# A trunk kernel's lead-in written in another order: the first coefficient group between the two input halves, the second half's squares summed on GpSimd and TensorE

## The chip, the core and the metric

The kernel runs on one core of a Trainium2 chip. A core has TensorE (PE, matrix products into PSUM, with a sequencer of its own for loading weights, PEld), VectorE (DVE), ScalarE (ACT), GpSimd (POOL), and SyncE (SP), on whose queue the loads and stores of this kernel are issued. The metric is the device time of one execution in microseconds (us).

## The reference

The reference is a decoder trunk of two layers on one sequence of 1024 tokens with 1024 channels. A layer normalizes its input, scales and shifts it by coefficients from a conditioning vector `c`, projects it once into all branches, runs three token mixers (pooling, retention, RWKV-7), merges them by gates and projects back:

```python
    mod = c_act @ w_ada + b_ada                       # c_act = silu(c)
    shift, scale, gate = jnp.split(mod[:, None, :], 3, axis=-1)
    h = rms_norm(x, norm_g) * (1.0 + scale) + shift
    proj = h @ w_in
    ...
    merged = jnp.sum(gates * y, axis=2)
    return x + gate * (merged @ w_out)
```

Here `rms_norm` multiplies x by the reciprocal root of the mean of its squares over the channels and by `norm_g`. All that the change touches is the first of these steps in the first layer: the sums of squares, the coefficients `scale` and `shift`, the normalized input `h`, and the first products with `w_in`.

## The kernel before

**Layout.** Activations lie with channels on the partitions: x is eight tiles (`kt` = 0 to 7, 128 channels each) by two halves (`h` = 0, 1, 512 tokens each), so a tile is 128x512. Matrix products contract over `kt`. They are made of three products each at the fast format: an operand is split into a rounded high part and a low remainder (`hhi`, `hlo` for h; `wh`, `wl`, or the two parts of a `wbig` tile, for weights), and high x high, low x high and high x low are added in one PSUM tile. ScalarE casts the high part, GpSimd or DVE subtracts for the low part (`split`, L529 and L530; `affine` and `low`, L1171 to L1177).

**The lead-in** is everything from the start to the end of the first layer's first three weight tiles (the low-rank tile and the first `k` and `r` tile of RWKV-7). It is written by hand: in `with tc.manual_schedule(...)` the order of the text is the order of each of PE, DVE, ACT and POOL; SP's order is placed by the compiler around it, and follows the text but for loads moved up from behind. Its pieces:

- `xdma(h, ...)` loads the tiles of half h; `wdma(j, ...)` the raw weights of the three tiles (j is the half of the contraction); `aload(g, n)` loads weights of coefficient group g into a ring of eight slots.
- `sq(h, ...)`: ScalarE squares a tile (L1127), DVE adds it to the running sum (L1131). `sums(h)`: four matmuls of 128x1 add that over the partitions. `rstd(h)`: ScalarE's root (L1146) and DVE's reciprocal (L1147). `rstd_bc(h)`: four matmuls broadcast the reciprocal roots to all partitions in PSUM (`rbc`). `rstd_copy(h)`: ScalarE copies this to SBUF (`rbs`, L1157), since GpSimd multiplies from there. `normed(h, kt, ...)`: x times the broadcast, on DVE from `rbc` (L1163) or on GpSimd from `rbs` (L1165).
- The coefficients come in groups. Groups 0 to 3 are scale and shift of tiles 0 to 3, group 4 of tiles 4 and 5, group 5 of tiles 6 and 7 (groups 6 and 7, the gates, come later and elsewhere). A group is a generator, `ada` (L225 and L227): eight steps, one per contraction tile, each a DVE instruction that multiplies a loaded weight tile by a column of `cact` and adds it to a sum in PSUM. `steps(g, n)` runs the next n of them. The ninth step is PE's column sums (`adaps`, 128x1 matmuls) and `ada_end`: DVE adds the bias (`mod`, L244) and makes the scale (`acoef`, L250).
- `affine(h, kt)`: two ScalarE passes make the high part and the full h (L1171, L1172); `low` its remainder (L1177). `mms(h, kt, tiles)`: the nine matmuls of one kt for three weight tiles (or those named), into the accumulators `acc6[h]`; those of half 0 come from the pool of accumulators (`acc_ps`), those of half 1 from the pools `ch` and `cy`, which serve the chunk work later, and the broadcast `rbc` earlier.
- `derive(l)`: four small DVE instructions on a vector of layer parameters (`vec`, L179 to L185).

A tile's h thus needs its half's reciprocal root and its group's coefficients; its matmuls need h and the split weights.

**Behind the lead-in** nothing is written out by hand: a planner keeps lanes of tasks, estimates times in a clock of its own that each recorded matmul advances, and gives out work by due time. The first task there evacuates the lead-in's accumulators; `setup_rest` loads the remaining constants and runs `derive(1)`, and `rope_tables` makes the rotary tables.

Of the kernel before, what the change touches and what calls it, by code (L numbers as in the profile page):

```python
# [13 lines left out]
ALU = mybir.AluOpType  # L14
# [3 lines left out]
P = 128  # L18
# [78 lines left out]
def trunk_kernel(ctx, tc, xT, cvec, pos, vecs, consts, w_ada, w_all, pool_w, lora_w, out):  # L97
# [79 lines left out]
    def derive(l):  # L177
        o = VEC["mu_k"]
        nc.vector.tensor_scalar(omu[l], vec[l][:, o : o + 13], -1.0, 1.0, op0=ALU.mult, op1=ALU.add)  # L179
        halved = vec[l][:, VEC["pool_scale"] : VEC["mu_k"]]  # L180
        nc.vector.tensor_scalar_mul(halved, halved, 0.5)
        o = VEC["k_k"]
        nc.vector.tensor_scalar_mul(vec[l][:, o : o + 4], vec[l][:, o : o + 4], -1.0)
        o = VEC["k_a"]
        nc.vector.tensor_scalar(oka[l], vec[l][:, o : o + 4], -1.0, 1.0, op0=ALU.mult, op1=ALU.add)  # L185

    def setup_rest():
        o = CST["bone"]
        braw = mo("braw")[:, 0:P]
        nc.sync.dma_start(out=braw, in_=consts[:, o : o + P])  # L190
        nc.vector.tensor_copy(bone, braw)
        nc.sync.dma_start(out=vec[1], in_=vecs[1])
        derive(1)

    def vv(l, k, i):
        o = VEC[k] + i
# [15 lines left out]
    def ada(l, g, slot_, gap=2200, acc_=t_lt, ws=None):  # L212
# [47 lines left out]
    def rope_tables():  # L260
# [10 lines left out]
        for h in range(2):  # L271
# [22 lines left out]
                nc.sync.dma_start(out=rope_d[h, 64 * r : 64 * r + 64, :], in_=n[0:64, :])  # L294
            nc.sync.dma_start(out=rope_d[2, 64 * h : 64 * h + 64, :], in_=n[64:128, :])
            yield 6000

    xd = [dp.tile([8, 2, P, HF], F32, name=f"xd{l}") for l in range(1)]
    gd = dp.tile([3, 8, 2, P, HF], F32, name="gd")
# [819 lines left out]
            nc.sync.dma_start(out=xt, in_=xT[kt, h])  # L1119
            xin[h].append(xt)  # L1120

    ssum = [None, None]

    def sq(h, *kts):
        for kt in kts:
            t = t_lt("sq") if kt == 0 else mo("sq")
            nc.scalar.square(t, xin[h][kt])  # L1127
            if kt == 0:
                ssum[h] = t
            else:  # L1130
                nc.vector.tensor_tensor(ssum[h], ssum[h], t, op=ALU.add)  # L1131

    ssp = [None, None]

    def sums(h):
        ssp[h] = mx("ssps")
        for m in range(4):
            mmul(ssp[h][:, m : m + 1], ssum[h][:, m * P : (m + 1) * P], ones)

    rn_ = [None, None]  # L1140
    rbc = [None, None]
# [65 lines left out]
    with tc.manual_schedule(engines={ET.PE, ET.DVE, ET.Activation, ET.Pool}):  # L1207
# [4 lines left out]
        def aload(g, n):  # L1212
            ada_load(0, g, wada_slot, aw[g], n)
# [35 lines left out]
        sq(1, 7)  # L1249
        sums(1)  # L1250
        wsp(0, 0)
        normed(0, 4, eng=G_)
        normed(0, 1)
        steps(gs[0], 6)
        rstd(1)
        steps(gs[0], 3)
        aload(3, 2)
        rstd_bc(1)
        wsp(0, 1, 2)
        steps(gs[1], 2)  # L1260
        affine(0, 0)
        steps(gs[1], 1)
        normed(1, 0)
        low(V, 0, 0)
# [4 lines left out]
        steps(gs[1], 3)
        rstd_copy(1)  # L1270
        acc6[0] = [acc_ps() for _ in range(3)]
        mms(0, 0)
        normed(1, 2, 3)
        acc6[1] = [ps_c.tile([P, HF], F32, tag=t, name=nm("acc"), bufs=n) for t, n in (("ch", 1), ("cy", 2), ("cy", 2))]
        mms(1, 0, 0, 1)
        steps(gs[1], 1)
        mms(1, 0, 2)
        normed(0, 5, 6, eng=G_)
        both(1)
        wdma(1, 0, 1, 2)  # L1280
        aload(4, 6)
        steps(gs[2], 8)
        mms(0, 1)
        mms(1, 1, 0, 1)
        steps(gs[2], 1)
        mms(1, 1, 2)
        wsp(1, 0)
        normed(0, 7, eng=G_)
        both(2)
        steps(gs[3], 8)  # L1290
        aload(4, 2)
        mms(0, 2)
        mms(1, 2, 0, 1)
        steps(gs[3], 1)
        mms(1, 2, 2)
        wsp(1, 1)
        both(3)
        wsp(1, 2)
        normed(1, 4, eng=G_)
        astep(4, 5)  # L1300
        mms(0, 3)
        mms(1, 3, 0, 1)
        steps(gs[4], 1)
        mms(1, 3, 2)
        both(4)
        normed(1, 5, eng=G_)
        both(5)
        astep(5)
# [323 lines left out]
```

## Time and profile before

| | |
|---|---|
| Time before, median of 3 runs | 2500.98 us (2497.89 to 2501.22) |
| Profiled execution, its own time | 2501.75 us |
| Its span, from first to last instruction | 2499.9 us |
| Mean granted TensorE clock | 0.983 |
| PE busy, of the span | 2397.6 us, 96% |
| DVE, ACT, POOL busy | 1357.1, 791.9, 822.8 us |
| First matmul of a weight tile | at 27.6 us |
| Last matmul of the lead-in ends; next weight tile begins | 77.4 us |

Times of the trace run from the start of the span. An instruction belongs to a line of the kernel; where a helper issues it, as `mmul` does for every matmul (L411), the tile names tell which it is: `ssps` are the column sums of squares, `rbc` the broadcast, `adaps` the column sums of a coefficient group, `acc` the accumulators of weight tiles. Idle time ahead of an instruction is put down to what released it.

### The profile page before, as it was taken

Reading aid. Unit: us, or ns where it says so; the run is one execution under the profiler, and the core shown is the slowest. Engines: PE = TensorE matmul, PEld = TensorE weight load, DVE = VectorE, ACT = ScalarE, POOL = GpSimd, SP = SyncE. Lnnn points to the kernel's source line nnn. Section 1 sums busy time; section 2 is a strip of 40 time slices with the busy share of each in tenths; the row PEclk is TensorE's granted clock in tenths of the full one; section 3 lists DMA queues with packets and bytes.
Section 4 is the critical chain, followed back from the end, with each engine's and each line's share of the span. In section 5 each row is a group of like instructions: output and inputs, shape, how many; then the busy total and the mean of one; then the engine's idle time right before and its main releaser. Section 6 shows DMA issues by size and latency. Waiting matters only on the chain. (4 is left out here: it accounts for less than half of the span.)

```text
span 2499.9 us, 34854 instructions
## 1 busy us (share of the span) xinstructions
PE 2397.6 (96%) x13312; PEld 1980.1 (79%) x13312; DVE 1357.1 (54%) x2564; ACT 791.9 (32%) x1465; POOL 822.8 (33%) x721
## 2 busy tenths in 40 slices
PE   6989999999999999999999999999999999999998
PEld 4778878877787787887877787788878778787888
DVE  7674566478268443567445646835744664412354
ACT  5532332231332222112444224223322322221243
POOL 4221322232133234454442132322313323236441
PEclk9999999999899999999999999999999999999999
DMA  7131112112113215676431211211211121354342
GB/s 245 54 109 56 43 35 85 36 38 68 47 55 115 75 57 161 193 230 190 136 112 47 68 39 34 77 35 43 86 42 35 61 81 55 123 156 126 102 152 77
DMA packets 124216, 223.68 MB, mean 89 GB/s; under 512 B 14096, under 2 KB 17424, under 8 KB 124048
## 3 DMA queue, kind: packets, MB, share of 16 engines
q1 hardware_dynamic: 124048, 221.44, 28.4%
q8 instruction: 105, 1.72, 0.3%
q14 instruction: 63, 0.52, 0.1%
HBM read 174.46 MB, written 46.92 MB: 89 GB/s over the span
## 5 line engine op out<-in xcount | busy, mean ns | idle before, releaser
L530 POOL TENSOR_TENSOR wl<-wr,wh 128x512 fp32r<-128x512 f32 x342 | 453.6, 1326 | 1189.5 <-ACT wh L529 1108.7
L411 PE MATMUL acc<-hhi,wh 128*128 128x512 f32 x2000 | 809.0, 404 | 14.5 <-DVE k L997 11.1
L411 PE MATMUL acc<-hhi,wl 128*128 128x512 f32 x2000 | 808.5, 404 | 1.7 <-POOL r L991 1.7
L411 PE MATMUL acc<-hlo,wh 128*128 128x512 f32 x2000 | 809.8, 405 | 0.0
L411 PEld LDWEIGHTS acc<-hhi,wh 128*128 128x128 f32 x2000 | 381.1, 191 | 86.5 <-DVE k L997 12.7
L411 PEld LDWEIGHTS acc<-hhi,wl 128*128 128x128 f32 x2000 | 381.4, 191 | 71.7 <-issue 2.2
L411 PEld LDWEIGHTS acc<-hlo,wh 128*128 128x128 f32 x2000 | 381.9, 191 | 68.3 <-issue 0.7
L529 ACT CAST wh<-wr 128x512 fp32r<-128x512 f32 x342 | 211.8, 619 | 680.8 <-PE acc L411 471.5
L411 PE MATMUL acc<-olo,wh 128*128 128x512 f32 x384 | 153.5, 400 | 4.4 <-POOL olo L530 4.3
L411 PE MATMUL acc<-oG,wh 128*128 128x512 f32 x384 | 153.3, 400 | 2.0 <-ACT oG L529 1.0
L411 PE MATMUL acc<-oG,wl 128*128 128x512 f32 x384 | 152.0, 396 | 0.0
L942 DVE TENSOR_TENSOR xst<-cy,MT 64x128 f32<-64x128 f32 x128 | 36.2, 283 | 185.5 <-PE cy L411 185.0
L953 DVE SCALAR_TENSOR_TENSOR S<-ch,pc,SP 64x64 f32<-64x64 f32 x256 | 72.4, 283 | 95.0 <-PE ch L411 86.1
L881 DVE TENSOR_TENSOR MT<-MT,tm 64x30 f32<-64x30 f32 (+14 forms) x240 | 103.9, 433 | 7.5
L939 ACT ACTIVATE SP<-S,pc 128x128 f32<-128x128 f32 x128 | 51.4, 402 | 173.8 <-DVE S L953 169.3
L875 DVE TENSOR_TENSOR tm<-MT 64x30 f32<-64x30 f32 (+14 forms) x240 | 101.3, 422 | 7.5
L948 DVE COPY Z<-ch 64x128 f32<-64x128 f32 x128 | 36.1, 282 | 117.7 <-PE ch L411 117.3
L411 PEld LDWEIGHTS acc<-olo,wh 128*128 128x128 f32 x384 | 73.2, 191 | 22.6 <-POOL olo L530 6.6
L411 PEld LDWEIGHTS acc<-oG,wh 128*128 128x128 f32 x384 | 72.9, 190 | 20.9 <-ACT oG L529 2.0
L1457 DVE SCALAR_TENSOR_TENSOR gs<-gs,acc 128x512 f32<-128x512 f32 x64 | 43.5, 683 | 82.8 <-PE acc L411 71.7
L411 PEld LDWEIGHTS acc<-oG,wl 128*128 128x128 f32 x384 | 73.1, 190 | 16.8
L411 PEld LDWEIGHTS ch<-xst,G 128*128 128x128 f32 x512 | 76.7, 191 | 11.6 <-DVE xst L942 0.5
(273 smaller groups left out, 3643.8 us busy)
## 6 DMA issues: line engine op xcount, KB each, us to landing
wr<-in_w_all SPq DMA_DIRECT2D x364, 256.0 KB, 2.7
gd<-gsg SPq DMA_DIRECT2D x80, 256.0 KB, 2.0
gs<-gd SPq DMA_DIRECT2D x80, 256.0 KB, 2.9
wada<-in_w_ada SPq DMA_DIRECT2D x70, 256.0 KB, 3.1
ol<-od SPq DMA_DIRECT2D x64, 256.0 KB, 3.0
ringG<-in_w_ada SPq DMA_DIRECT2D x26, 256.0 KB, 5.2
x<-in_xT SPq DMA_DIRECT2D x16, 256.0 KB, 4.9
od<-po SPq DMA_DIRECT2D x16, 256.0 KB, 2.3
```

Source lines behind the costliest of these rows:

```text
L411: nc.tensor.matmul(out, lhsT=lhsT, rhs=rhs, start=start, stop=stop, **kw)
L529: nc.scalar.copy(hi, src)
L530: eng.tensor_tensor(lo, src, hi.bitcast(F32), op=ALU.subtract)
L875: nc.vector.tensor_tensor(pr, M3[:, i + 1 :, i : i + 1].to_broadcast([64, n, i]), M3[:, i : i + 1, 0:i].to_broadcast([64, n, i]), op=ALU.mult,
L881: nc.vector.tensor_tensor(M3[:, i + 1 :, 0:i], M3[:, i + 1 :, 0:i], pr, op=ALU.add)
L939: nc.scalar.activation(SP, S, AF.Copy, scale=pcc)
L942: nc.vector.tensor_tensor(xst[0:64, :], cy[0:64, 0:P], AV[:, c * P : (c + 1) * P], op=ALU.add)
L948: nc.vector.tensor_copy(Z[0:64, c, :], ch[0:64, 0:P])
L953: nc.vector.scalar_tensor_tensor(Sn[rw, rw], ch[rw, P + 64 * hd : P + 64 * hd + 64], pc[rw, c : c + 1], SP[rw, rw], op0=ALU.mult, op1=ALU.add,
L1457: nc.vector.scalar_tensor_tensor(s, s, 1.0, ps, op0=ALU.add, op1=ALU.mult)
```

## The change

Five things are done differently in the lead-in, and two small pieces of text are moved.

1. Loads: group 0's four weight tiles are issued ahead of half 1's eight input tiles; the first three raw weight tiles come together behind half 1.
2. Half 1's squares (`sq2`): ScalarE squares two tiles, GpSimd adds the pair, and PE adds the pair's column sums into one PSUM tile, four times. DVE makes half 0's sum alone. Both halves' sums go into tiles of the accumulators' pool.
3. Group 0 is computed between the halves. In `ada` a step is added between the column sums and `ada_end`, so that the next group's two first steps can be put between them, and they are for groups 1 to 5.
4. Normalization: tiles 2 and 3 of half 0 go from GpSimd to DVE; tiles 6 and 7 of half 1 from DVE to GpSimd; of tile 1, the low part of half 0 is on DVE. Tiles 6 and 7 of half 1 are normalized before the matmuls of tile 4, and no longer behind them.
5. Matmuls: half 0 and half 1 alternate to the end, where before tiles 6 and 7 of half 0 came first and then those of half 1; and they are less cut up by weight tile.

The load of the second layer's parameter vector and `derive(1)` are moved from `setup_rest` to the end of `rope_tables`. The diff, cut to its core:

```diff
@@ setup_rest, ada, rope_tables
-        nc.sync.dma_start(out=vec[1], in_=vecs[1])
-        derive(1)
...
             mmul(ps[:, m : m + 1], acc[:, m * P : (m + 1) * P], ones)
+        if not late:
+            yield
         ada_end(l, g, ps)
...
             yield 6000
+        nc.sync.dma_start(out=vec[1], in_=vecs[1])
+        derive(1)
@@ lead-in
-    def sq(h, *kts):
+    def sq(*kts):
...
-    def sums(h):
-        ssp[h] = mx("ssps")
+    def sums():
+        ssp[0] = acc_ps()
...
+    def sq2(j):
+        a, b = mo("sq"), t_lt("sq")
+        nc.scalar.square(a, xin[1][2 * j])
+        nc.scalar.square(b, xin[1][2 * j + 1])
+        nc.gpsimd.tensor_tensor(a, a, b, op=ALU.add)
+        if j == 0:
+            ssp[1] = acc_ps()
+        for m in range(4):
+            mmul(
+                ssp[1][:, m : m + 1], a[:, m * P : (m + 1) * P], ones,
+                start=(j == 0 and m == 0), stop=(j == 3 and m == 3), skip_group_check=True,
+            )
...
+        aload(0, 4)
         xdma(1, *range(8))
-        wdma(0, 0)
-        aload(0, 4)
-        wdma(0, 1, 2)
+        wdma(0, 0, 1, 2)
         aload(1, 4)
...
-        sq(0, *range(8))
-        sums(0)
-        sq(1, 0, 1, 2)
+        sq(*range(8))
+        sums()
+        steps(gs[0], 4)
+        sq2(0)
         rstd(0)
         rstd_bc(0)
         derive(0)
-        sq(1, 3, 4, 5, 6)
+        steps(gs[0], 4)
+        aload(3, 2)
+        sq2(1)
+        steps(gs[0], 1)
+        sq2(2)
+        steps(gs[0], 1)
         rstd_copy(0)
-        normed(0, 2, 3, eng=G_)
         normed(0, 0)
...
+        affine(0, 0)
         normed(0, 1)
-        steps(gs[0], 6)
+        sq2(3)
+        wsp(0, 0, 1, 2)
+        low(V, 0, 0)
+        normed(0, 2, 3)
+        steps(gs[1], 5)
         rstd(1)
...
         mms(0, 4)
         mms(1, 4)
-        normed(1, 6, 7, eng=V)
         mms(0, 5)
-        mms(1, 5, 0, 1)
         steps(gs[5], 1)
-        mms(1, 5, 2)
+        mms(1, 5)
+        steps(gs[5], 1)
         both(6, V)
         both(7, V)
         wprep(True)
         wprep()
         mms(0, 6)
+        mms(1, 6)
         mms(0, 7)
-        mms(1, 6)
         mms(1, 7)
```

**How the instructions now stand.** DVE, from the last addition to half 0's sum (`sq_183`) on; before:

```order
L1131 TENSOR_TENSOR sq_183<-sq_183,sq_203 128x512
L1131 TENSOR_TENSOR sq_211<-sq_211,sq_213 128x512
L1131 TENSOR_TENSOR sq_211<-sq_211,sq_216 128x512
L1147 RECIPROCAL rn_219<-rn_219 128x4
L179 TENSOR_SCALAR omu_103<-vec_91 128x13
L181 TENSOR_SCALAR vec_91<-vec_91 128x28
L183 TENSOR_SCALAR vec_91<-vec_91 128x4
L185 TENSOR_SCALAR oka_105<-vec_91 128x4
L1131 TENSOR_TENSOR sq_211<-sq_211,sq_231 128x512
L1131 TENSOR_TENSOR sq_211<-sq_211,sq_234 128x512
L1131 TENSOR_TENSOR sq_211<-sq_211,sq_237 128x512
L1131 TENSOR_TENSOR sq_211<-sq_211,sq_240 128x512
```

and with the change:

```order
L1134 TENSOR_TENSOR sq_183<-sq_183,sq_203 128x512
L223 TENSOR_SCALAR ada_ps_212<-ringG_137,cact 128x256
L225 SCALAR_TENSOR_TENSOR ada_ps_212<-ringG_137,cact,ada_ps_212 128x256 x3
L1161 RECIPROCAL rn_227<-rn_227 128x4
L179 TENSOR_SCALAR omu_103<-vec_91 128x13
L181 TENSOR_SCALAR vec_91<-vec_91 128x28
L183 TENSOR_SCALAR vec_91<-vec_91 128x4
L185 TENSOR_SCALAR oka_105<-vec_91 128x4
L225 SCALAR_TENSOR_TENSOR ada_ps_212<-ringG_137,cact,ada_ps_212 128x256 x3
L225 SCALAR_TENSOR_TENSOR ada_acc_211<-ringG_137,cact,ada_ps_212 128x256
L244 TENSOR_TENSOR mod_99<-adaps_254,vec_91 128x2
L250 SCALAR_TENSOR_TENSOR acoef_101<-mod_99,vec_91 128x1
```

Half 1's additions (`sq_211`) are gone from DVE; four of group 0's steps stand ahead of half 0's reciprocal and four behind `derive(0)`, and group 0's coefficient (`mod_99`, `acoef_101`) ahead of the first normalization.

PE from its first instruction; before:

```order
L411 MATMUL ssps_206<-fixed,sq_183 128x1 x4
L411 MATMUL rbc_222<-cst,rn_219 128x128 x4
L411 MATMUL ssps_251<-fixed,sq_211 128x1 x4
L411 MATMUL adaps_273<-fixed,ada_acc_260 128x1 x2
L411 MATMUL rbc_280<-cst,rn_268 128x128 x4
L411 MATMUL acc_313<-hhi_293,wbig_153 128x512 x2
```

and with the change (`acc_206` and `acc_222` are the halves' column sums now):

```order
L413 MATMUL acc_206<-fixed,sq_183 128x1 x4
L413 MATMUL acc_222<-fixed,sq_217 128x1 x4
L413 MATMUL rbc_230<-cst,rn_227 128x128 x4
L413 MATMUL acc_222<-fixed,sq_245 128x1 x4
L413 MATMUL adaps_254<-fixed,ada_acc_211 128x1 x2
L413 MATMUL acc_222<-fixed,sq_257 128x1 x4
L413 MATMUL acc_222<-fixed,sq_276 128x1 x4
L413 MATMUL acc_319<-hhi_271,wbig_158 128x512 x2
L413 MATMUL acc_319<-hlo_272,wbig_158 128x512
L413 MATMUL rbc_325<-cst,rn_301 128x128 x4
L413 MATMUL adaps_330<-fixed,ada_acc_294 128x1 x2
```

Half 1's column sums became four pieces, two of which stand ahead of group 0's column sums (`adaps_254`); the second broadcast (`rbc_325`) and group 1's column sums stand behind the first weight tile's three matmuls of tile 0.

DVE in groups 2 and 3; before (`ada_ps_369` is group 2, `ada_ps_415` group 3, `vec_92` the second layer's parameters):

```order
L227 SCALAR_TENSOR_TENSOR ada_ps_369<-wada_177,cact,ada_ps_369 128x256
L227 SCALAR_TENSOR_TENSOR ada_acc_368<-wada_177,cact,ada_ps_369 128x256
L244 TENSOR_TENSOR mod_99<-adaps_393,vec_91 128x2
L250 SCALAR_TENSOR_TENSOR acoef_101<-mod_99,vec_91 128x1
L225 TENSOR_SCALAR ada_ps_415<-wada_179,cact 128x256
L227 SCALAR_TENSOR_TENSOR ada_ps_415<-wada_179,cact,ada_ps_415 128x256
L227 SCALAR_TENSOR_TENSOR ada_ps_415<-wada_181,cact,ada_ps_415 128x256 x2
L227 SCALAR_TENSOR_TENSOR ada_ps_415<-ringG_156,cact,ada_ps_415 128x256 x2
```

and with the change (group 2 is `ada_ps_334`, group 3 `ada_ps_409`):

```order
L225 SCALAR_TENSOR_TENSOR ada_ps_334<-wada_177,cact,ada_ps_334 128x256
L225 SCALAR_TENSOR_TENSOR ada_acc_333<-wada_177,cact,ada_ps_334 128x256
L179 TENSOR_SCALAR omu_104<-vec_92 128x13
L181 TENSOR_SCALAR vec_92<-vec_92 128x28
L183 TENSOR_SCALAR vec_92<-vec_92 128x4
L185 TENSOR_SCALAR oka_106<-vec_92 128x4
L223 TENSOR_SCALAR ada_ps_409<-wada_179,cact 128x256
L225 SCALAR_TENSOR_TENSOR ada_ps_409<-wada_179,cact,ada_ps_409 128x256
L244 TENSOR_TENSOR mod_99<-adaps_396,vec_91 128x2
L250 SCALAR_TENSOR_TENSOR acoef_101<-mod_99,vec_91 128x1
```

`derive(1)`, though its text was moved behind, is placed right behind group 2 here and was placed amid group 3 before; group 2's coefficient now has two steps of group 3 ahead of it.

More of the change, by code (lines that the diff above doesn't have):

```diff
@@ L1120, in xdma @@
             xin[h].append(xt)
-    ssum = [None, None]
-    def sq(h, *kts):
+    ssum = []
+    ssp = [None, None]
+    def sq(*kts):
         for kt in kts:
             t = t_lt("sq") if kt == 0 else mo("sq")
-            nc.scalar.square(t, xin[h][kt])
+            nc.scalar.square(t, xin[0][kt])
             if kt == 0:
-                ssum[h] = t
+                ssum.append(t)
             else:
-                nc.vector.tensor_tensor(ssum[h], ssum[h], t, op=ALU.add)
-    ssp = [None, None]
-    def sums(h):
-        ssp[h] = mx("ssps")
+                nc.vector.tensor_tensor(ssum[0], ssum[0], t, op=ALU.add)
+    def sums():
+        ssp[0] = acc_ps()
         for m in range(4):
-            mmul(ssp[h][:, m : m + 1], ssum[h][:, m * P : (m + 1) * P], ones)
+            mmul(ssp[0][:, m : m + 1], ssum[0][:, m * P : (m + 1) * P], ones)
+    def sq2(j):
[10 more added lines that the diff above has]
+            )
     rn_ = [None, None]
@@ L1244, in trunk_kernel @@
         derive(0)
-        sq(1, 3, 4, 5, 6)
+        steps(gs[0], 4)
[4 more added lines that the diff above has]
+        steps(gs[0], 1)
         rstd_copy(0)
-        normed(0, 2, 3, eng=G_)
         normed(0, 0)
[L1249 to L1252, printed above, removed]
+        affine(0, 0)
         normed(0, 1)
-        steps(gs[0], 6)
-        rstd(1)
-        steps(gs[0], 3)
-        aload(3, 2)
+        sq2(3)
+        wsp(0, 0, 1, 2)
@@ L1258, in trunk_kernel @@
+        low(V, 0, 0)
+        normed(0, 2, 3)
+        steps(gs[1], 5)
+        rstd(1)
+        steps(gs[1], 3)
+        wdma(1, 0, 1, 2)
+        aload(4, 6)
+        acc6[0] = [acc_ps() for _ in range(3)]
+        mms(0, 0, 0)
         rstd_bc(1)
-        wsp(0, 1, 2)
-        steps(gs[1], 2)
-        affine(0, 0)
         steps(gs[1], 1)
+        steps(gs[2], 2)
         normed(1, 0)
-        low(V, 0, 0)
+        steps(gs[1], 1)
+        normed(0, 4, 5, eng=G_)
         affine(1, 0)
-        steps(gs[1], 2)
+        rstd_copy(1)
@@ L1267, in trunk_kernel @@
         normed(1, 1)
         low(V, 1, 0)
[L1269 to L1272, printed above, removed]
+        affine(0, 1)
+        affine(1, 1)
+        steps(gs[2], 2)
+        low(V, 0, 1)
         normed(1, 2, 3)
+        low(G_, 1, 1)
         acc6[1] = [ps_c.tile([P, HF], F32, tag=t, name=nm("acc"), bufs=n) for t, n in (("ch", 1), ("cy", 2), ("cy", 2))]
[L1275 to L1282, printed above, removed]
+        mms(0, 0, 1, 2)
+        mms(1, 0)
+        steps(gs[2], 4)
+        normed(1, 4, eng=G_)
         mms(0, 1)
-        mms(1, 1, 0, 1)
         steps(gs[2], 1)
-        mms(1, 1, 2)
+        mms(1, 1)
+        steps(gs[3], 2)
+        steps(gs[2], 1)
+        both(2)
         wsp(1, 0)
-        normed(0, 7, eng=G_)
-        both(2)
-        steps(gs[3], 8)
+        normed(1, 5, eng=G_)
+        steps(gs[3], 6)
@@ L1291, in trunk_kernel @@
         aload(4, 2)
         mms(0, 2)
-        mms(1, 2, 0, 1)
         steps(gs[3], 1)
-        mms(1, 2, 2)
-        wsp(1, 1)
+        mms(1, 2)
+        steps(gs[4], 2)
+        steps(gs[3], 1)
         both(3)
-        wsp(1, 2)
-        normed(1, 4, eng=G_)
-        astep(4, 5)
+        wsp(1, 1, 2)
+        normed(0, 6, eng=G_)
+        aload(5, 2)
+        for _ in range(6):
+            steps(gs[4], 1)
+            aload(5, 1)
         mms(0, 3)
-        mms(1, 3, 0, 1)
+        mms(1, 3, 0)
@@ L1303, in trunk_kernel @@
         steps(gs[4], 1)
-        mms(1, 3, 2)
+        mms(1, 3, 1, 2)
+        steps(gs[5], 2)
+        steps(gs[4], 1)
         both(4)
-        normed(1, 5, eng=G_)
+        normed(1, 6, eng=G_)
         both(5)
-        astep(5)
+        normed(0, 7, eng=G_)
+        normed(1, 7, eng=G_)
+        steps(gs[5], 6)
         mms(0, 4)
         mms(1, 4)
-        normed(1, 6, 7, eng=V)
         mms(0, 5)
-        mms(1, 5, 0, 1)
         steps(gs[5], 1)
-        mms(1, 5, 2)
+        mms(1, 5)
+        steps(gs[5], 1)
```

## The prediction, as it was made before the changed kernel was run

> **What bounds the kernel now.** I read the page's busy shares first, then busy time by stretches of the lead-in (start and end in us, length, then busy time and instruction count of PE, PEld, DVE, ACT and POOL, the granted clock, DMA share, GB/s).
>
> ```profile
> PE 2397.6 (96%) x13312; PEld 1980.1 (79%) x13312; DVE 1357.1 (54%) x2564; ACT 791.9 (32%) x1465; POOL 822.8 (33%) x721
> 0.00:27.61 27.61, 8.71 (x37) 7.98 (x37) 18.19 (x39) 16.05 (x28) 11.18 (x17) 1.00 0.96 340
> 27.61:56.49 28.88, 23.65 (x92) 16.47 (x93) 24.12 (x51) 14.83 (x21) 14.47 (x14) 0.94 0.56 189
> 56.49:77.45 20.96, 19.90 (x80) 15.25 (x81) 11.85 (x18) 15.76 (x24) 10.39 (x8) 0.92 0.10 35
> ```
>
> PE is the bound of the whole, so the lead-in is worth exactly what it moves the moment when PE runs without gaps. Three stages: until 27.61 PE has no work worth naming; until 56.49 it waits in bits for coefficients, DVE being busy 24.12 of 28.88 us; from 56.49 (first matmul of contraction tile 4) PE is full and needs 20.96 us to the next weights' tile at 77.45. I therefore follow DVE's chain to the end of coefficient group 4, then the hand-off to PE, then PE's tail. The timeline of DVE (start, duration, instructions; in brackets the idle time before and its releaser):
>
> ```profile
> 8.61 3.08 DVE L1131 TENSOR_TENSOR sq<-sq,sq 128x512 f32<-128x512 f32 x4 [0.18 <-ACT sq L1127]
> 12.86 1.49 DVE L1131 TENSOR_TENSOR sq<-sq,sq 128x512 f32<-128x512 f32 x2 [1.17 <-ACT sq L1127]
> 14.27 0.17 DVE L1147 RECIPROCAL rn<-rn 128x4 f32<-128x4 f32 x1
> 14.41 0.17 DVE L181 TENSOR_SCALAR vec<-vec 128x28 f32<-128x28 f32 x1
> 14.69 3.07 DVE L1131 TENSOR_TENSOR sq<-sq,sq 128x512 f32<-128x512 f32 x4
> 18.28 1.16 DVE L1131 TENSOR_TENSOR sq<-sq,sq 128x512 f32<-128x512 f32 x1
> 19.36 0.67 DVE L1163 TENSOR_TENSOR x<-x,rbc 128x512 f32<-128x512 f32 x1
> 20.47 2.59 DVE L227 SCALAR_TENSOR_TENSOR ada_ps<-ringG,cact,ada_ps 128x256 f32<-128x256 f32 x5
> 25.27 0.16 DVE L244 TENSOR_TENSOR mod<-adaps,vec 128x2 f32<-128x2 f32 x1 [1.17 <-PE adaps L411]
> 25.46 1.24 DVE L250 SCALAR_TENSOR_TENSOR acoef<-mod,vec 128x1 f32<-128x1 f32 x1
> 28.66 0.69 DVE L1177 TENSOR_TENSOR hlo<-x,hhi 128x512 fp32r<-128x512 f32 x1
> 40.99 0.16 DVE L244 TENSOR_TENSOR mod<-adaps,vec 128x2 f32<-128x2 f32 x1 [2.56 <-PE adaps L411]
> 44.92 1.26 DVE L181 TENSOR_SCALAR vec<-vec 128x28 f32<-128x28 f32 x1
> 48.46 4.71 DVE L227 SCALAR_TENSOR_TENSOR ada_ps<-ringG,cact,ada_ps 128x512 f32<-128x512 f32 x6
> 53.21 0.75 DVE L227 SCALAR_TENSOR_TENSOR ada_acc<-ringG,cact,ada_ps 128x512 f32<-128x512 f32 x1
> ```
>
> The reader is to see two things: DVE idles 1.17 and 2.56 us for PE's column sums, and one small instruction (L181) takes 0.17 us at 14.41 but 1.26 at 44.92. GpSimd's timeline says why:
>
> ```profile
> 25.43 2.49 POOL L1165 TENSOR_TENSOR x<-x,rbs 128x512 f32<-128x512 f32 x2
> 44.86 1.30 POOL L1177 TENSOR_TENSOR hlo<-x,hhi 128x512 fp32r<-128x512 f32 x1 [0.27 <-ACT x L1172]
> ```
>
> A DVE instruction that reads and writes SBUF alone and starts while GpSimd runs a two-operand pass waits for the end of that pass: 44.92 + 1.26 = 46.18 against 44.86 + 1.30 = 46.16. The coefficient steps, which add into PSUM, pass unhindered (2.59 for five, with GpSimd busy).
>
> **The change, part by part: DVE up to group 4.** From 8.61 + 3.08 = 11.69 (half 0 summed) to 53.21 + 0.75 = 53.96 DVE needs 42.27 us.
>
> Taken off: the additions for half 1, 1.49 + 3.07 + 1.16 = 5.72. Waits that go: 1.17 for squares, 1.17 and 2.56 for column sums, 4.90, the last because two steps of the next group now stand ahead of each coefficient. Blocked time that goes, since GpSimd is idle there in the new order: 1.24 - 0.16 and 1.26 - 0.17, 2.17. Put on: normalization of two tiles that GpSimd did (2 x 0.67) and one low part (0.69), 2.03.
>
> New waits, from these rows of SP (issue), PE and ACT:
>
> ```profile
> 5.97 5.46 SPq L1119 DMA_DIRECT2D x<-in_xT  x8
> 11.75 1.87 PE L411 MATMUL ssps<-fixed,sq 128*128 128x1 f32 x8 [11.75 <-DVE sq L1131]
> 14.49 2.07 PE L411 MATMUL rbc<-cst,rn 128*128 128x128 f32 x8 [0.88 <-DVE rn L1147]
> 24.25 0.99 PE L411 MATMUL adaps<-fixed,ada_acc 128*128 128x1 f32 x4 [2.89 <-DVE ada_acc L227]
> 11.46 2.04 ACT L1127 ACTIVATE sq<-x 128x512 f32<-128x512 f32 x3 [0.80 <-DMA x<-in_xT]
> 26.74 0.81 ACT L1171 ACTIVATE hhi<-x,mod,acoef 128x512 fp32r<-128x512 f32 x1 [4.06 <-DVE acoef L250]
> 30.94 0.59 ACT L1157 COPY rbs<-rbc 128x512 f32<-128x512 f32 x1 [0.50 <-DVE x L1163]
> ```
>
> (1) Four weight loads now precede half 1 on SP. Eight loads take 5.46, so half 1 comes 4 x 0.68 = 2.7 later and its first square runs at 11.46 + 2.7 = 14.2. ScalarE's root for half 0 is queued behind the first pair of squares: reciprocal at 15.7, while DVE has done its four new steps at 11.69 + 4 x 0.52 = 13.8. Wait 1.9.
>
> (2) GpSimd's additions run from 15.6 to 19.6, three of about 1.28 back to back (2.49 for two in the row above). Reciprocal and the four instructions of derive(0) are SBUF alone and fall into just that time. Between 0 (all slip through, as three of them did at 44 to 47) and three times (1.28 - 0.15) = 3.4; I take 3.4, because at 44.92 the like instruction waited for the whole rest.
>
> (3) PE is in order: ahead of group 0's column sums stand two pairs' square sums (1.87 each by the 11.75 row) and the broadcast (2.07), from 16.9 on. Column sums done at 16.9 + 1.87 + 2.07 + 1.87 + 0.99 = 23.7; DVE is ready at 21.7. Wait 2.0. At full clock the pair sums cost about half, wait 0.
>
> (4) The low part of tile 0 waits for two ScalarE passes (0.81 each): 1.2 beyond the normalization beside it.
>
> (5) In half 1 the copy of the broadcast stands behind both passes of the first tile, and DVE's second normalization waits for it (ScalarE and DVE take turns on that tile, 30.94 row): 0.81 + 0.84 + 0.59 less what DVE does meanwhile, 1.7.
>
> (6) Coefficients of groups 1 and 3 and the second reciprocal meet GpSimd's passes: 0.4 + 1.1 + 0.5 = 2.0, bounds 0 and 3.4; group 2's wait for its column sums, 0.6.
>
> Sum of the new waits 1.9 + 3.4 + 2.0 + 1.2 + 1.7 + 2.0 + 0.6 = 12.8. Net: -5.72 - 4.90 - 2.17 + 2.03 + 12.8 = +2.0. Group 4 ends at about 56.0. First matmul: weight splits stand behind the last pair of squares on ScalarE and GpSimd, near 30 instead of 27.6; no price, since DVE sets what follows.
>
> **Hand-off and tail.** PE's rows:
>
> ```profile
> 33.05 0.58 PE L411 MATMUL adaps<-fixed,ada_acc 128*128 128x1 f32 x4 [0.80 <-DVE ada_acc L227]
> 56.49 2.93 PE L411 MATMUL acc<-hhi,wbig 128*128 128x512 f32 x6 [0.57 <-ACT hhi L1171]
> 60.14 1.55 PE L411 MATMUL acc<-hhi,wbig 128*128 128x512 f32 x6
> 62.21 1.52 PE L411 MATMUL acc<-hhi,wbig 128*128 128x512 f32 x6
> 64.25 1.07 PE L411 MATMUL acc<-hhi,wbig 128*128 128x512 f32 x4
> 65.63 0.95 PE L411 MATMUL adaps<-fixed,ada_acc 128*128 128x1 f32 x8
> 67.87 1.67 PE L411 MATMUL acc<-hhi,wbig 128*128 128x512 f32 x6 [0.48 <-ACT hhi L1171]
> 70.98 1.67 PE L411 MATMUL acc<-hhi,wbig 128*128 128x512 f32 x6 [0.58 <-ACT hhi L1171]
> 36.00:40.00 4.00, 4.00 (x13) 0.60 0.00 0
> ```
>
> From group 4's last step to its first matmul: 56.49 - 53.96 = 2.53. Now two steps of group 5 come first (2 x 0.79 = 1.57, and the column sums run meanwhile), then mod 0.16, coefficient 0.16 to 0.9, ScalarE 0.81 and 0.1: about 3.1, +0.6. Tile 4 then starts at 56.49 + 2.0 + 0.6 = 59.1.
>
> The tail was 20.96. Nine matmuls take 64.25 - 62.21 = 2.04 at full clock; the first nine took 60.14 - 56.49 = 3.65, at half clock. Eight nines are 16.3, group 5's column sums 0.95 (65.63 row), the waits at 67.87 and for the first low part 0.5 each: 18.2. The wait at 70.98 goes, as the last tiles are normalized earlier and the halves alternate. But half 0's accumulators now finish one nine before the end instead of two, and ScalarE has three weight casts ahead of reading them: +0.5. Tail 18.7, bounds 18.2 and, with the half clock again (3.65 - 2.04 = 1.6), 20.3. PE goes on at 59.1 + 18.7 = 77.8, against 77.45: **+0.35 us**.
>
> On that half clock: in the last row above the clock was 0.60 although PE's longest pause just ahead was 0.80 us (33.05). The Trainium skill (TensorE: Matmul & The Clock Gate, Why this matters for your kernels) warns of idle gaps over about 3 us between bursts. By that rule the tail, without such a gap, stays at full clock (18.7); by the rows a half-idle stretch is enough, and it may fall there (20.3).
>
> The vecs[1] load and derive(1), moved behind the rope tables in the text, stand in the built order still inside the lead-in, behind group 2: price 0.
>
> **Behind the lead-in** the planner's clock starts a little differently, and PE's order differs in places through layer 0, from where head 0's chunk work begins. Its largest waits from 77.45 to 1050:
>
> ```profile
> PE rot L417 <- DVE yc L675: 12.8, 7, 3.7
> PE pps L411 <- ACT pdh L529: 4.1, 1, 4.1
> PE pps L411 <- ACT MT L902: 3.9, 1, 3.9
> ```
>
> No instruction is added there, so I take 0; one such wait more or less is 4.1 either way.
>
> **Sum.** 2501.75 (this execution, span 2499.9 and 1.85 around it) + 0.35 = 2502.1. This execution lies 0.77 above the median of the runs, 2500.98, so against the runs the forecast is 2501.3, 2501.
>
> **Rivals.** *The order works as its row of hand-offs reads* (chance 0.26): (2), (3) and (5) do not come, coefficients of group 0 stand four us earlier and the lead is kept. 0.35 - 3.4 - 2.0 - 1.7 = -6.75: 2494. For it: three of five small instructions slipped through before; DVE has 5.72 us less to do. Against: seven waits must vanish together, and each engine is in order. It decides if tile 4 starts before 54.
>
> *Half 1's third accumulator holds PE* (0.20): it takes the PSUM slot of a broadcast and so waits for half 1's fourth normalization, near 40.9; group 2's column sums are queued behind. PE idles 4 us there; at full clock the 0.6 of (6) is all that DVE feels of it. At half clock the fourteen matmuls ahead of the column sums take 14 x (2.93 - 1.52) / 6 = 3.3 longer, all of it waited for by DVE; the tail's half clock adds 1.6, and one more blocked coefficient 0.9: 0.35 + 3.3 + 1.6 + 0.9 = +6.1: 2507. For it: both half-clock stretches before came behind such bits. It decides if group 2's coefficients come after 47.
>
> *The new order behind the lead-in draws more or fewer waits*: inside the likeliest case, as above.
>
> **How the numbers follow.** Likeliest case 0.54, own range 2496 to 2506 (lead-in -2 to +2, waits behind it up to 4). This kernel's measurement tells 0.2%, 5 us, from no change. From the likeliest case 0.46 lies within, 0.04 on each side; the first rival gives 0.23 faster and 0.03 within; the second 0.15 slower and 0.05 within. So 0.27 faster, 0.54 same, 0.19 slower. The range for 8 in 10 takes in most of both rivals: 2493 to 2508.
>
> **What would show it.** Right: reciprocal of half 0 near 15.7 and derive(0) taking over 1 us beside GpSimd's additions; group 0's coefficient near 24, group 4's last step at 54 to 57; tile 4's first matmul at 57 to 61; gapless matmuls from 76 to 79. Wrong: DVE's small instructions at 0.17 throughout, tile 4 before 54, or PE's waits in layer 0 differing by over 5 us from the 34 of before.

## The result: slower, behind the lead-in

The changed kernel took 2524.76 us (median of 4 runs, 2522.36 to 2527.27) against 2501.10 for the kernel before (4 runs, 2497.89 to 2507.41): a ratio of 1.0070, 95% interval 1.0043 to 1.0098. Forecast were 2501 and a range of 2493 to 2508. In two longer comparisons later the ratio was 1.0043 (1.0028 to 1.0059; 2518.23 against 2508.24 us) and 1.0067 (1.0046 to 1.0088; 2521.29 against 2502.57 us). The change is slower: by 10 to 24 us between the medians of the three comparisons, and by about 10 us once TensorE's clock is set apart (last column of the table below). Ratios and intervals are those on record with the runs; where single runs spread widely they differ from the quotient of the two medians (1.0095 in the first comparison).

Single executions of one and the same kernel spread here: the kernel before took 2494.2 to 2524.2 us in 109 runs. What follows therefore rests on medians of many runs, and on two quantities of a profile that tell apart what belongs to a kernel and what to one execution.

**The lead-in did what was forecast.** By stretches of the changed kernel (start and end, length, then busy time and count of PE, PEld, DVE, ACT and POOL, granted clock, DMA share, GB/s), cut at its own first matmul of a weight tile, its first matmul of tile 4 and the hand-over to the next weights:

```profile
0.00:29.83 29.83, 11.43 (x52) 11.26 (x53) 17.08 (x37) 16.51 (x27) 7.73 (x16) 1.00 0.88 317
29.83:59.92 30.09, 24.37 (x101) 18.76 (x102) 24.37 (x51) 14.09 (x21) 18.00 (x15) 0.94 0.58 185
59.92:78.21 18.29, 17.74 (x80) 14.25 (x81) 7.67 (x13) 14.71 (x23) 11.66 (x12) 1.00 0.07 18
```

The clock's record begins at 33.3 us, so the 1.00 of the first row is not measured. Tile 4 starts at 59.92 (forecast 59.1), the tail takes 18.29 at full clock (18.7), and PE goes on at 78.2 (77.8), where it was 77.45. In this profile the lead-in cost 0.8 us and not 24. DVE's and GpSimd's timelines show the steps:

```profile
15.62 0.18 DVE L1161 RECIPROCAL rn<-rn 128x4 f32<-128x4 f32 x1 [2.01 <-ACT rn L1160]
15.71 1.13 DVE L179 TENSOR_SCALAR omu<-vec 128x13 f32<-128x13 f32 x1
16.92 1.24 DVE L185 TENSOR_SCALAR oka<-vec 128x4 f32<-128x4 f32 x1
23.00 0.16 DVE L244 TENSOR_TENSOR mod<-adaps,vec 128x2 f32<-128x2 f32 x1 [2.89 <-PE adaps L413]
42.26 0.17 DVE L185 TENSOR_SCALAR oka<-vec 128x4 f32<-128x4 f32 x1
55.75 0.75 DVE L225 SCALAR_TENSOR_TENSOR ada_acc<-ringG,cact,ada_ps 128x512 f32<-128x512 f32 x1
```

```profile
15.51 1.26 POOL L1145 TENSOR_TENSOR sq<-sq,sq 128x512 f32<-128x512 f32 x1 [14.29 <-ACT sq L1144]
16.87 2.68 POOL L1145 TENSOR_TENSOR sq<-sq,sq 128x512 f32<-128x512 f32 x2
```

The reciprocal stands at 15.62 behind a wait of 2.01 (forecast 15.7 and 1.9). Two of derive(0)'s four instructions take 1.13 and 1.24 instead of about 0.16, because they started while GpSimd added squares. Group 4's last step ends at 56.5 (56.0).

**Where the time went.** PE's idle time behind the lead-in is the length of a stretch less its busy time. From 77.45 to 1230 us, layer 0, of the kernel before, and of the changed one (length, PE's busy time and count, clock, DMA share, GB/s):

```profile
77.45:1230.00 1152.55, 1114.39 (x6192) 0.98 0.31 95
```

```profile
77.45:1230.00 1152.55, 1104.94 (x6112) 0.97 0.30 93
```

That is 38.2 us idle before and 47.6 now: 9.4 us that come from the order of layer 0, although no instruction was added there. PE's waits in it, changed kernel (what waits and its line, what is waited for; us in total, times, longest):

```profile
PE rot L419 <- DVE yc L677: 11.3, 7, 3.6
PE acc L413 <- ACT gsg L1072: 10.7, 2, 8.2
PE pps L413 <- ACT pdh L531: 5.1, 1, 5.1
```

In the profile of the kernel before, the same wait is small:

```profile
PE acc L411 <- ACT gsg L1070: 3.4, 2, 2.8
```

One wait of 8.2 us is new. What stands around it, on PE, on DVE and on ACT:

```profile
633.28 0.80 PE L413 MATMUL acc<-hhi,wh 128*128 128x512 f32 x1 [8.19 <-ACT gsg L1072]
```

```profile
625.75 1.97 DVE L887 STREAM_TRANSPOSE MT<-MT 32x1024 f32<-32x1024 f32 x1
627.61 3.75 DVE L892 STREAM_TRANSPOSE G<-MT 32x1024 f32<-32x1024 f32 x2
631.39 0.69 DVE L638 SCALAR_TENSOR_TENSOR pd<-pt,pu 128x512 f32<-128x512 f32 x1
```

```profile
632.12 0.62 ACT L531 CAST pdh<-pd 128x512 fp32r<-128x512 f32 x1 [14.71 <-DVE pd L638]
632.64 0.59 ACT L1072 ACTIVATE gsg<-acc 128x512 f32<-128x512 f32 x1
633.64 0.60 ACT L1072 ACTIVATE gsg<-acc 128x512 f32<-128x512 f32 x1
```

The pooling mixer's cast `pdh` waits for DVE's `pd`, which stands behind three transposes of another mixer. ScalarE is in order: it sits idle for 14.71 us, and queued behind the cast are two evacuations (`gsg`) of accumulators that PE needs for its next weight tile.

**The rest is TensorE's clock.** The record of the granted clock holds stretches at half, in multiples of 3.41 us. Such a step of 3.41 us is called a window here. In the kernel before there were 26 windows at half clock (half windows), in the profile of the changed one 36, and two stretches alone took seven each, at 214 and at 2068 us. Around the first (window, length, PE's busy time and count, granted clock, DMA share, GB/s):

```profile
207.38:210.80 3.42, 3.42 (x16) 1.00 0.38 140
210.80:214.21 3.41, 3.41 (x69) 1.00 0.49 156
214.21:217.62 3.41, 3.41 (x32) 0.50 0.01 3
...
234.69:238.10 3.41, 3.41 (x11) 0.50 0.00 0
238.10:241.52 3.42, 3.42 (x20) 1.00 0.00 0
```

PE is busy all the time, and yet the clock falls. The same windows for the tile `m` alone, 32x32 matmuls of the RWKV-7 solve:

```profile
210.80:214.21 3.41, 2.39 (x64) 1.00 0.49 156
214.21:217.62 3.41, 1.45 (x27) 0.50 0.01 3
```

The window ahead of the fall held two whole groups of them, 64 matmuls and 2.39 of 3.41 us. These two quantities, idle time of PE and half-clock windows (each costs half of PE's busy time in it), account for all times here: span less idle less half-clock loss is 2362 to 2372 us in sixteen profiles of all kernels below but the dense one, where it is 2351. Before: 2499.9 - 102.3 - 34.3 = 2363.3. Changed: 2525.5 - 111.1 - 50.3 = 2364.1. Of the 25.6 us between these two profiles, 8.8 are idle time and 16.0 half clock.

### The profile page after: what moved, and what is told of

It reads as the page before. It is cut to its first block, busy times and chain, and to the rows that moved or that the text cites. A ratio compares the mean times of both kernels' runs of the same rounds, so it can differ in the third digit from the quotient of the medians.

```text
span 2525.5 us, 34896 instructions
## 1 busy us (share of the span) xinstructions
PE 2414.4 (96%) x13336; PEld 1995.2 (79%) x13336; DVE 1353.9 (54%) x2558; ACT 790.4 (31%) x1465; POOL 823.5 (33%) x724
## 5 line engine op out<-in xcount | busy, mean ns | idle before, releaser
L877 DVE TENSOR_TENSOR tm<-MT 64x30 f32<-64x30 f32 (+14 forms) x240 | 108.7, 453 | 7.4
L883 DVE TENSOR_TENSOR MT<-MT,tm 64x30 f32<-64x30 f32 (+14 forms) x240 | 98.8, 412 | 7.7
L413 PEld LDWEIGHTS ch<-xst,G 128*128 128x128 f32 x512 | 76.7, 191 | 11.5 <-DVE xst L944 0.3
```

The costliest lines, as they stand in the source:

```text
L413: nc.tensor.matmul(out, lhsT=lhsT, rhs=rhs, start=start, stop=stop, **kw)
L877: nc.vector.tensor_tensor(pr, M3[:, i + 1 :, i : i + 1].to_broadcast([64, n, i]), M3[:, i : i + 1, 0:i].to_broadcast([64, n, i]), op=ALU.mult,
L883: nc.vector.tensor_tensor(M3[:, i + 1 :, 0:i], M3[:, i + 1 :, 0:i], pr, op=ALU.add)
```

## Experiments

Idle is PE's from 77.45 to 1230 us, half windows are those of the whole profile; both from one profiled execution of each kernel. The last two columns are estimates from all runs: each run's span and mean granted clock are on record (for the kernel before in 105 runs), and span times (1 - clock) is what the run lost to the clock. Within one kernel, a run that lost 1 us more was 0.79 us longer, and that leaves a standard deviation of 1.7 us where the spans of the kernel before have 5.9. "Apart" is the mean span less that of the kernel before, with 0.79 of the difference in lost time taken off; it is good to about 1 us for 10 runs or more, and less well for fewer.

| kernel | ratio to before (95%) | idle, us | half windows | lost to the clock, us | apart, us |
|---|---|---|---|---|---|
| before; again | 1 | 38.2; 36.0 | 26; 30 | 45 | 0 |
| changed, first comparison | 1.0070 (1.0043 to 1.0098) | 47.6 | 36 | 57 (4 runs) | +9.9 |
| changed, again (one run) | - | 47.8 | 24 | 40 | +9.9 |
| changed, longer | 1.0043 (1.0028 to 1.0059) | 46.5 | 24 | 48 | +10.7 |
| changed, beside the late cast | 1.0067 (1.0046 to 1.0088) | 47.7 | 31 | 50 (6 runs) | +11.5 |
| old lead-in, derive(1) moved | 1.0026 (1.0009 to 1.0043) | 47.6 | 31 | 44 | +9.1 |
| new lead-in, derive(1) back | 1.0003 (0.9985 to 1.0021) | 37.7 | 28 | 45 | +1.4 |
| as that, charge of 300 ns | 0.9996 (0.9972 to 1.0019) | 36.9 | 24 | 44 | +0.3 |
| charge of 600 ns | 1.0017 (0.9998 to 1.0036) | 34.7 | 23 | 47 | 0.0 |
| charge of 2000 ns | 1.0058 (1.0035 to 1.0082) | 49.4 | 28 | 48 | +11.9 |
| changed, one cast three places later | 1.0013 (0.9994 to 1.0032) | 40.0 | 36 | 41 | +4.4 |
| before, small groups spaced | 0.9938 (0.9919 to 0.9956) | 32.2 | 22 | 35 (6 runs) | -4.4 |
| new lead-in, derive(1) back, spaced | 0.9955 (0.9937 to 0.9973) | 34.7 | 22 | 37 (7 runs) | -1.8 |
| whole change, spaced | 1.0009 (0.9988 to 1.0029) | 42.5 | 27 | 44 | +4.7 |
| before, only 32x32 groups spaced | 1.0023 (1.0005 to 1.0041) | 38.6 | 24 | 42 | +10.6 |
| before, small groups dense | 1.0027 (1.0008 to 1.0045) | 46.0 | 31 | 55 | +3.5 |

### The two halves of the change apart

The change has a new lead-in, and four small instructions (derive(1)) whose text moved. Each alone:

```diff
 def setup_rest():
...
         nc.vector.tensor_copy(bone, braw)
-        nc.sync.dma_start(out=vec[1], in_=vecs[1])
-        derive(1)
...
 def rope_tables():
...
             yield 6000
+        nc.sync.dma_start(out=vec[1], in_=vecs[1])
+        derive(1)
```

in the kernel before,

> The kernel before, with one edit of the change alone: the load of the second layer's parameters and derive(1) stand at the end of the rope tables. The order of all engines behind the lead-in is then exactly that of the changed kernel, the lead-in that of before. Theory A (the 24 us come from the planner's other order in layer 0, by way of TensorE's clock, which fell to half at 214 us for 23.9 us where two groups of 32x32 matmuls came close together): 2515 to 2526. Theory B (the new lead-in itself, by moving all later work by about 1 us): 2499 to 2503. If both halves are needed: in between.

and undone in the changed kernel:

> The changed kernel with the load of the second layer's parameters and derive(1) put back into setup_rest: the new lead-in, and behind it the order of before on every engine. Theory A: 2501 to 2503 (the lead-in's own +0.9 us). Theory B: 2518 to 2526. A third, that a half-clock stretch falls by chance of the phase: anything from 2498 to 2515 with runs of one kernel spread by more than 8 us.

Measured were 2511.95 us (12 runs) and 2507.99 (12 runs) beside 2507.45 for before. The idle time goes wholly with derive(1), 47.6 against 37.7; by its ratio the new lead-in alone is not distinguishable from no change. Theory A holds on the place, not on the size: the medians lie 4.5 us apart, where 14 or more were expected (2515 beside 2501), and apart from the clock the move costs 9.1 us. The rest of the first 24 is clock: the four runs of the first comparison lost 57 us to it, those of the two longer ones 48 and 50. The same two kernels once more, for second profiles:

> The kernel before once more, for a second profile. If the stretches of half clock belong to the order of the work, the same ones come at the same places (582, 626, 800, 824 in layer 0, none of over 14 us); if they come by chance of the clock's windows, others come.

> The changed kernel once more, for a second profile. Order: the stretches of 23.9 us at 214 and 2068 come again at the same places, time 2522 to 2527. Chance of the windows: at least one of the two is missing or elsewhere, each worth 8 to 9 us.

2507.34 us and 2511.16. The kernel before, which had no long stretch at 2040, now had one of seven windows there; the changed one had neither of its two. The four stretches of layer 0 that the expectation names, all behind waits, came again 2 us earlier (580, 624, 798, 822) and as long. The long stretches are thus chance of one execution; those behind waits and the idle time are not (idle 36.0 and 47.8). The longer comparison settles the size:

> The changed kernel timed again beside the kernel before, in more runs, since runs of one kernel have spread over 20 us (before: 2495.9 to 2517.3). Theory A (two parts: the moved derive(1) permutes layer 0 and adds 10 us of idle TensorE there, 47.7 against 37.3 us between 77 and 1230 us; the rest of the first +24 was half-clock windows that fell badly): median 8 to 12 us above before, runs spread over 15 us. Theory B (the +24 belongs to the order as a whole): 20 to 26 us above. Theory C (all chance): within 4 us.

The median is 10.0 us above before, as in theory A, with runs from 2508.8 to 2524.9.

### What the moved text does

With the new lead-in, the four instructions of derive(1) run at 42 us in both places of the text (at 41.98 in the changed kernel, at 41.54 with the text put back), and at 44.4 and 44.9 with the old one: in the built order they stand inside the lead-in either way. What moved is the planner's account. It charges 944 ns of VectorE time when the text is passed, and once that charge falls at the end of the rope tables, other tasks are given out in another order. With derive(1) back in its place and only a charge at that point, the built order of all engines is that of the changed kernel at 944 ns, and another one at other charges (300 here, 600 and 2000 in two further kernels):

```diff
             yield 6000
+        settle()
+        idle_at[ET.DVE] = max(idle_at[ET.DVE], clock[0]) + 300
```

> The changed kernel with derive(1) put back into setup_rest, and the planner told, at the end of the rope tables, that VectorE is busy for 300 ns more (no instruction is added). With 944 ns in its place the order is exactly that of the changed kernel. Theory A: each such charge gives another order of layer 0, whose idle TensorE (77 to 1230 us) lies anywhere from 33 to 50 us; time within 12 us of before on either side. Rival (less charge, less loss): idle in between, 40 to 44 us.

> The same with a charge of 2000 ns. Theory A: idle anywhere from 33 to 50 us, not in step with the charge. Rival (the loss grows with the charge): over 48 us idle, 2525 or more.

> The changed kernel with derive(1) put back and a charge of 600 ns on VectorE at the end of the rope tables. In its order the cast stands behind the evacuations, as at 300. Theory A (this one place carries most of the loss): no wait of 8 us near 627, idle TensorE from 77 to 1230 us under 41, time within 4 us of before. Rival (the loss grows with the charge): 42 to 45 us idle.

2504.47 us (before beside it 2502.83), 2520.75 (2502.83) and 2507.78 (2502.57). At 300 and 600 ns the idle time is that of before, at 944 and 2000 it is 10 us more. Neither "anywhere" nor "in step with the charge" describes these four charges: there is one step, between 600 and 944. The built orders on its two sides differ in many places (600 and 2000 ns differ in 262 of ScalarE's 1470). One of them is the cast `pdh` on ScalarE: behind the two `gsg` at 300 and 600, ahead of them at 944 and 2000. What it alone is worth, the next experiment shows.

### One instruction three places later

```diff
-            yield 2400
+            yield 2400 + 1000 * ((l, g, h) == (0, 2, 1))
             dh, dl = t_mo("pdh", F32R)[:, 0:HF], t_mo("pdl", F32R)[:, 0:HF]
             split(d, dh, dl, nc.vector)
```

This changes one thing in the built program, on ScalarE: the cast moves behind three instructions (the expectation counts four places). Changed kernel, then this one:

```
L531 CAST pdh_5192<-pd_5179            L1072 ACTIVATE gsg_5193<-acc_5119
L1072 ACTIVATE gsg_5197<-acc_5119      L531 CAST wh_4998<-wr_5000
L531 CAST wh_4998<-wr_5000             L1072 ACTIVATE gsg_5196<-acc_5120
L1072 ACTIVATE gsg_5200<-acc_5120      L531 CAST pdh_5217<-pd_5179
```

> The changed kernel with 1000 ns more between the pooling mixer's difference and its cast, for one group and half (group 2, half 1 of layer 0). In the built order one instruction moves: on ScalarE the cast pdh stands four places later, behind the two evacuations (gsg) that it stood ahead of. All other engines' orders are identical. Theory A (the evacuations waited behind this cast, and TensorE for them): the 8.1 us wait near 627 us falls to under 3, idle TensorE from 600 to 870 us from 21 to 13 or 15, and the time by 6 to 8 us, to about 2510 where the changed kernel has 2518. Rival (TensorE would wait there for the chain of 32x32 matmuls anyway, which starts from the same transposes): the wait turns into one for MT or G of 4 us or more, gain under 4 us.

> The changed kernel beside it: 8 to 12 us above before, 6 to 8 above the kernel with the late cast (theory A), or under 4 above it (rival).

2506.05 us (12 runs) against 2521.29 (6 runs) on the same chip. PE's waits of the kernel with the late cast, and its stretch:

```profile
PE rot L419 <- DVE yc L677: 11.2, 7, 3.6
PE pps L413 <- ACT pdh L531: 5.1, 1, 5.1
PE acc L413 <- ACT gsg L1072: 4.0, 2, 2.5
```

```profile
77.45:1230.00 1152.55, 1112.55 (x6148) 0.98 0.30 94
```

The 8.2 us are gone, and idle time falls by 7.7, from 47.7 to 40.0. No wait took its place: the chain of 32x32 matmuls, the rival, starts at 631.4 us behind the same transposes, and PE has other work until then. The medians differ by 15 us, more than the idle time explains: these twelve runs lost 41 us to the clock and the six beside them 50. Apart from the clock the difference is 7.1 us (11.5 against 4.4). So this one place makes up more than half of the loss; the other 4 us, in the rest of the new order, were not traced.

### The half clock

The granted clock's windows lie on a grid of 3.41 us that stands differently to the program in each execution. Most falls stand behind waits. In seventeen profiles 250 full-clock windows are followed by half clock, and 196 of them are partly idle ones without 32x32 matmuls and column sums of 128x1: of such windows all 158 with PE busy for under 1.4 us fell, of those from 1.4 to 1.8 us 38 of 89, and of the 10,793 with more, none. The pauses need not be long: in 110 of the 196 none reached 3 us, and at 2250 to 2283 us two pauses of 1.04 us were enough, in the kernel before (2258) as in most others.

The others hold small matmuls. There are some 10,800 windows at full clock with PE busy for over 3.3 us; 17 of them are followed by half clock. Each of the 17 held 2.19 us or more of 32x32 matmuls. Of the windows with 2.3 us or more, 13 of 14 fell; of those from 2.1 to 2.3, 4 of 35; of the others, none. Once at half clock, the groups take 1.91 us instead of 1.19, and windows with such groups, or then with 64x64 ones for 2 us or more, keep it there: for up to seven windows, and in one profile (derive(1) moved alone, at 1843) for ten. At full clock, two windows with over 3 us of 64x64 matmuls did not lower it.

The Trainium skill (TensorE: Matmul & The Clock Gate, What's actually happening) gives a free-running window of 3413 ns, so that the moment of a change of the clock depends on where in the window the work falls; the profiles agree, with stretches of one to seven times 3.41 us and one of ten. It has the clock fall after an idle window, and this fall needs none.

If two groups in a window do it, wider gaps must prevent it (the first gap stands behind a group of 32x32 matmuls and is there twice, the second behind one of 64x64):

```diff
-                    yield 600
+                    yield 1600
...
-            yield 400
+            yield 1200
```

> The kernel before, with the gaps that the planner is told to leave behind each group of 32x32 matmuls raised from 600 to 1600 ns and behind each group of 64x64 matmuls from 400 to 1200: some eight 128x512 matmuls between groups instead of three to five. Theory A (a window of 3.41 us in which two such groups fall sets the clock to half although TensorE is busy throughout, and the groups that follow keep it there): no half-clock stretch begins behind a window in which TensorE was busy all the time, none is over 14 us, and half-clock windows fall from 25 to 30 to 18 to 22; about 5 us faster than before, less what the other order adds in idle. Rival (the stretches follow from waits and from chance): as many stretches as before, among them ones of over 14 us in some executions, time unchanged or slower by the later recurrence.

> The changed kernel with derive(1) put back and the wider gaps: new lead-in, no permuted layer 0 by derive(1), fewer half-clock stretches. Theory A: as the spaced kernel before within 2 us, 2500 to 2505. If the new lead-in were worth something of its own, it would show here as a difference to the spaced kernel before.

2493.04 us (6 runs, spread 7 us) and 2497.45 (7 runs) beside 2508.24 for before, which spread 21 us. Windows around the first solve in the spaced kernel before, all of PE, and then tile `m` alone:

```profile
208.94:212.35 3.41, 3.41 (x43) 1.00 0.38 102
212.35:215.76 3.41, 3.41 (x50) 1.00 0.16 57
215.76:219.18 3.42, 3.42 (x54) 1.00 0.00 0
```

```profile
208.94:212.35 3.41, 1.24 (x33) 1.00 0.38 102
212.35:215.76 3.41, 1.44 (x41) 1.00 0.16 57
215.76:219.18 3.42, 1.45 (x46) 1.00 0.00 0
```

No window holds more than 1.45 us of them, and the clock stays. No fall behind 32x32 matmuls is left in either profile, and no stretch over 14 us. This is the fastest version, 0.62% under before, and it beats both kernels. It gains 15 us where about 5 were expected. Not all of that is the clock: the other order also has less idle time, 32.2 against 36 to 38, and by the runs' clocks 4.4 us of the gain are the order's. The new lead-in lies 4.4 us above the old one here, outside the 2 us of its expectation, and has 2.4 us more idle time behind it: a wait at 154 us is 4.1 us long there and 1.4 with the old one. Apart from the clock it costs 2.6 us.

> The kernel before, with these gaps set to 0, so that two groups of 32x32 matmuls (2.3 us) and four of 64x64 (4.6 us) stand side by side. Theory A: half-clock stretches behind fully busy windows in at least five of the eight heads (four in each layer), half-clock windows 35 to 50, 8 to 20 us slower than before. Rival (only idle TensorE lowers the clock): no such stretch, and the time within 4 us of before or faster, since the chain comes earlier.

2517.73 us, in the expected range, and yet a miss: no stretch began behind a fully busy window, and there were 31 half windows where 35 to 50 were expected. Four 64x64 groups side by side do not lower the clock, and two adjoining 32x32 groups (2.3 us) fall whole into one window in one case of three ((3.41 - 2.3) / 3.41). Idle time rose, to 46.0 us in layer 0, but the ten runs say that most of the loss is the clock's after all: they lost 55 us to it, where the kernel before lost 48 beside them, and apart from the clock this kernel is 3.5 us slower. In its profile the clock was down for six windows each behind two partly idle windows (at 842 and 2040) with 1.4 and 1.3 us of 32x32 matmuls in them; whether the other runs lost the time in that way was not seen. The reverse, 32x32 groups alone spaced:

> The kernel before with the wider gap (1600 ns) behind the groups of 32x32 matmuls alone; the groups of 64x64 stay at 400. Theory A (a window with over 0.65 of 32x32 work lowers the clock, 64x64 work alone does not, as windows with 1.0 of it stayed at full clock): no half-clock stretch behind a fully busy window, 20 to 24 half-clock windows, and a time within 4 us of the kernel with both gaps widened, 2493. Rival (the 64x64 groups matter as much): stretches of over 14 us remain in the profile, 2500 or more.

2513.41 us. On the clock it is as expected, no fall behind a fully busy window and 24 windows; on the time it is not. Its order of layer 1 is another one, in which PE waits more (1230 to 2400 us, this kernel, then before):

```profile
1230.00:2400.00 1170.00, 1129.34 (x6243) 0.98 0.23 73
```

```profile
1230.00:2400.00 1170.00, 1139.04 (x6308) 0.99 0.25 76
```

40.7 us idle against 31.0: what the clock gave, one order took (apart from the clock, 10.6 us slower than before). Last, the whole change with both gaps:

> The whole change, derive(1) moved as in it, with the wider gaps behind the groups of 32x32 and 64x64 matmuls. The order of layer 0 is another one again. Theory A (the 10 us of idle TensorE are an accident of one order, not a price of the move): idle TensorE from 77 to 1230 us within 5 us of the 34.7 of the spaced kernel with derive(1) put back, and 2491 to 2503, spread under 10 us. Rival (moving derive(1) costs in any order): about 10 us above 2497.

2508.11 us, beside 2502.83 for before. Idle time is 42.5, or 7.8 above the spaced kernel with derive(1) put back, and the time is nearer to the rival's. The charge thus cost 8 to 10 us of idle time in two different families of orders (apart from the clock 9.3 and 6.5 us), in the second by other waits (5.6 us in two at 844 to 851, 6.1 in two at 998 to 1009). Whether a late charge tends to give worse orders, or these were two accidents, stays open.

## Why the prediction was wrong

By its own steps:

- **DVE up to group 4, hand-off and tail: right.** Sum +0.35 us; the profile shows +0.8, and the runs apart from the clock 1 to 3 us. Part of the agreement is luck, since errors of the terms cancel: (1) was 2.01 for 1.9, (3) 2.89 for 2.0, with group 0's sums done at 23.0 where 23.7 was forecast; (2) was over-sized, two blocked instructions and about 2.0 us instead of three and 3.4; (4) was 1.13 for 1.2, (5) 1.88 for 1.7, and of (6) group 2's wait was 2.24 for 0.6. The tail ran at full clock, 18.29 us.
- **"The vecs[1] load and derive(1) ... price 0": the step that failed.** It looked at where the instructions stand, which was right, and not at what the planner charges for them. The charge of 944 ns at another point is the whole reason for the other order: alone, with no instruction moved, it gives the changed kernel's order on every engine, and the move alone, in the kernel before, costs 9.1 us apart from the clock.
- **"No instruction is added there, so I take 0; one such wait more or less is 4.1 either way": mis-sized.** The prediction saw that PE's order differs from head 0's chunk work on. The term measured 9.4 us of idle time, 7.7 of them by one ScalarE instruction. The bound came from the longest wait shown, but an in-order queue can join two waits: here a cast that waits for DVE and an evacuation that PE waits for. The sign by which it would be wrong, waits in layer 0 differing by over 5 us, came.
- **The clock: seen in the lead-in alone.** The rule on long idle gaps and the half-idle stretches were weighed for 20 us of tail, while 26 windows over the whole program were at half clock, and their number differs by up to twelve between executions of the same kernel (24 to 36 in the changed one). That a half-idle stretch is enough, as the prediction read from its rows, is what all profiles bear out. A difference of 5 us was called what a measurement tells; 3 runs on one chip don't tell that here.
- **The rivals.** The first (2494) fell: tile 4 started at 59.9, not before 54. The second had its wait, PE held 4.19 us by half 1's fourth normalization at 40.24, as it had placed it near 40.9, and the clock was at half behind it, from 40.13 to 43.54. But DVE waited 2.24 us for group 2's column sums, not the 0.6 + 3.3 of that rival, and the coefficient stood at 45.6 and not behind 47, so it did not decide. The third, which the prediction folded into its likeliest case, was the one that came.

## What to carry to other kernels

Where a planner with modelled costs sets the order, an edit is not priced by its instructions alone: compare the built orders to the end of the program, and where they differ, look in each in-order queue for an instruction that waits ahead of one that is waited for. Read idle time of the bounding engine and the clock's loss apart before comparing two times; the first repeats between executions, the second does not, and here its differences are as large as the effect. The granted clock of every run, where it is on record, does that without a profile. Groups of small matmuls belong between large ones with enough distance that no window of 3.41 us holds two.

## What the runs showed of the hardware

TensorE's clock fell to half behind every window of 3.41 us with less than 1.4 us of work, and behind none that had over 1.8 us of it and no small matmuls. It also fell behind windows in which it was busy throughout, where 32x32 matmuls took 2.2 us or more of 3.41; 64x64 matmuls, up to a whole window of them, did not do it. Column sums of 128x1 seem to belong to the first kind: in the spaced kernel before one fall, at 1008 us, came behind a window with 3.29 us busy, 1.84 of it such sums. That was not tried apart, and 32 windows with the same 1.84 us and no idle time stayed at full clock. A fall costs from one window to ten, by what follows: at half clock a window with 0.7 of 128x512 matmuls kept the clock down in one profile (221.04 in the changed kernel) and let it rise in another (216.71 in the kernel before), so the point at which it rises lies near that, with some weight for what fills the rest.
